# Seven-product form for the output projection and for the whole second MLP product, adding DMAs for low parts, and operand tiles moved by 32 bytes, in a gated two-branch trunk

## The chip, the cores and the metric

The kernel runs on one core of a Trainium2 chip. The metric is the device time of one execution in microseconds (us). Three runs of the kernel before took 847.4, 850.44 and 851.98 us; their median is 850.44 us.

## The reference

One layer over 512 tokens of 1024 channels, all in float32, with a final norm behind it:

```python
h = rmsnorm(x, norm_mix[l])
proj = h @ w_in[l]
zu, zv, zq, zf, zi, zo, g_a, g_b = jnp.split(proj, split_points, axis=-1)
y_a = gmlp_branch(zu, zv, ...) @ w_up_a[l]
y_b = hgrn2_branch(zq, zf, zi, zo, ...) @ w_up_b[l]
mix = jax.nn.sigmoid(g_a) * y_a + jax.nn.sigmoid(g_b) * y_b
x = x + mix @ w_out[l]
h = rmsnorm(x, norm_ffn[l])
x = x + jnp.square(jax.nn.relu(h @ w_ff1[l])) @ w_ff2[l]
...
return rmsnorm(x, final_norm)
```

`w_out` is 1024x1024 and `w_ff2` is 4096x1024. These two products, and the norm between the projection and the MLP, are what the change touches.

## The kernel before

**Precision.** Each float32 operand is split into a high part H and a low part L, both in the type float32r. `split` (L87 to L90) writes H by a copy on ScalarE (ACT, L89) and L = source - H by a subtraction on VectorE (DVE, L90). `mm3` (L106 to L115) then does three matmuls for each pair of blocks: H by H (L113), L by H and H by L (L114, L115), summed in PSUM. `operand` splits a weight tile of 128x1024 into the tiles WH and WL, two rings of NOPER = 5 buffers each; `wload` also loads the tile, in the order of a list (`_plan`), through a ring of four tiles named raw.

**Seven products.** Where a product is cut into 2x2 blocks it can be done in seven block products with sums of blocks before and after, in place of eight. `seven` (L117 to L157) does this for the branch gates and for most of the first MLP product; the loop at L721 to L791 does it for chunks 1 to 3 of the second one. A chunk is eight blocks of 128 hidden channels, and its 168 matmuls of 128x512 are seven products of 24. Its inner function `product` (L748) splits an activation quarter into aH and aL, splits two weight tiles and calls `mm3`. Two of the weight sums, w1 and w3, come from DRAM ready: a DMA from SyncE's queue (SP) writes one quarter and a second DMA, issued by GpSimd (POOL), adds another one:

```python
nc.sync.dma_start(t, rows(*parts[0], k))
if len(parts) > 1:
    nc.gpsimd.dma_start(t, rows(*parts[1], k), accum_op=ALU.add)
```

**Plain products.** The output projection (L612 to L623) and chunk 0 of the second MLP product (L670 to L682) are plain: 192 matmuls of 128x512 each. In the projection the operands mixH and mixL were split tile by tile inside the `upb` loop (L585 to L592); each of the eight results is added to x2 by one DVE addition (L619), squared for the norm on ACT, and in the second half `norm_to_T` (L222 to L235) normalises a token tile, transposes it on TensorE (PE) and splits it into h2H and h2L.

**After the projection** the first MLP product does its first four blocks plainly (L635 to L644), in two halves of 256 tokens, and 14 pairs by `seven`. Then follow chunk 0, chunks 1 to 3 and the final norm.

**Order.** Each engine runs its own instructions in one fixed order, which the framework's list scheduler derives at build time (L876) from the program and the pools. A tile's address comes from the order in which pools hand out tiles.

Of the kernel before, what the change touches and what calls it, by code (L numbers as in the profile page):

```python
# [29 lines left out]
NSLOW = 8  # L30
# [15 lines left out]
def _plan():  # L46
# [15 lines left out]
    for hf in range(2):  # L62
        names += [("out", hf, k) for k in range(4)]
    names += [("ff1", f) for f in range(NF)]
    names += [("ff2", f) for f in range(NSLOW)]
    for c in range(NSLOW // 8, NF // 8):
        names += [("ff2q", c, j, l, k) for j, l in QUARTERS for k in range(2)]
# [4 lines left out]
def trunk_kernel(ctx: ExitStack, tc: tile.TileContext, A: dict, out: bass.AP):  # L72
# [7 lines left out]


# [10 lines left out]
    def operand(src):  # L92
        n = src.shape[-1]
        H = wp.tile([P, 1024], F32R, tag="WH", bufs=NOPER, name="WH")
        L = wp.tile([P, 1024], F32R, tag="WL", bufs=NOPER, name="WL")
        split(src, H[:, :n], L[:, :n])
        return H, L

    def wload(*name):
        return operand(wraw(*name))  # L100
# [81 lines left out]


# [64 lines left out]
    yaL = pya.tile([P, NG, S], F32R, name="yaL")  # L248

# [314 lines left out]
    pt = left2.enter_context(tc.tile_pool(name="pt", bufs=1, side="left", reuse_waits="tile"))  # L564
    ps_g = left2.enter_context(tc.tile_pool(name="ps_g", bufs=1, space=bass.MemoryType.PSUM))
# [17 lines left out]
    mixH = pmix.tile([P, KD, S], F32R, name="mixH")  # L583
    mixL = pmix.tile([P, KD, S], F32R, name="mixL")
    for d in range(KD):  # L585
# [5 lines left out]
        nc.vector.tensor_tensor(sb, part[0][:, d, :], sb, ALU.add)  # L591
        split(sb, mixH[:, d, :], mixL[:, d, :])  # L592
# [9 lines left out]
    pr3 = left2.enter_context(tc.tile_pool(name="pr3", bufs=1, side="left", reuse_waits="tile"))  # L602
    h2H = pr3.tile([P, KD, S], F32R, name="h2H")
# [8 lines left out]
    for hf in range(2):  # L612
        W = [wload("out", hf, k) for k in range(4)]
        cs = slice(hf * 512, (hf + 1) * 512)
        for t in range(NT):
            acc = ps.tile([P, S], F32, tag="acc", bufs=2, name="acc")
            tt = slice(t * P, (t + 1) * P)
            mm3(acc, [((mixH[:, k, tt], mixL[:, k, tt]), blk(W[k // 2], k % 2, 512)) for k in range(KD)])
            nc.vector.tensor_tensor(x2[:, t, cs], x2[:, t, cs], acc, ALU.add)  # L619
            junk = pn.tile([P, S], F32, tag="junk", bufs=1, name="junk")  # L620
            mean_square(junk, x2[:, t, cs], ssq2[:, t, hf:hf + 1])
            if hf == 1:
                norm_to_T(pn, x2[:, t, :], t, ssq2[:, t, :], [gbc2[:, :S], gbc2[:, S:]], h2H, h2L)  # L623
# [3 lines left out]
    pn_stack.close()  # L627
# [34 lines left out]
    eight = [b for pool, tag in ((ps, "hm"), (ps, "acc"), (ps2, "y5"), (ps2, "y3")) for b in banks(pool, tag)]  # L662
    aT, W2 = {}, {}

    def ff2(f, t, hf):
        tt = slice(t * P, (t + 1) * P)
        mm3(eight[2 * t + hf], [((aT[f][0][:, tt], aT[f][1][:, tt]), blk(W2[f], hf, 512))],
            (f == 0, f == NSLOW - 1))

    for f in range(NSLOW):  # L670
        aT[f] = operand(act[f])
        W2[f] = wload("ff2", f)
        if f < NSLOW - 2:
# [14 lines left out]
    ms = po2.tile([P, NT, 2], F32, name="ms")  # L690

    def add_to(l, m, src):

        for i in range(2):
            c = x2[:, 2 * l + i, m * S:(m + 1) * S]
            nc.vector.tensor_tensor(c, c, src[i], ALU.subtract if m else ALU.add)
# [24 lines left out]
    for c in range(NSLOW // 8, NF // 8):  # L721
        one, end = c == NSLOW // 8, c == NF // 8 - 1
        def rows(j, l, k):
            return A["w"][index[("ff2q", c, j, l, k)]]

        def fresh(pool, tag, bufs, *parts):

            ts = [pool.tile([P, 1024], F32, tag=tag, bufs=bufs, name=tag) for k in range(2)]
            for k, t in enumerate(ts):
                nc.sync.dma_start(t, rows(*parts[0], k))  # L730
                if len(parts) > 1:
                    nc.gpsimd.dma_start(t, rows(*parts[1], k), accum_op=ALU.add)
            return ts

        b11 = fresh(wp, "raw", 4, (0, 0))
        w1 = fresh(wp, "raw", 4, (0, 1), (0, 0))
        b22 = fresh(po2, "rawx", 6, (1, 1))
        w4 = fresh(po2, "rawx", 6, (1, 0))  # L740
        w3 = fresh(po2, "rawx", 6, (1, 1), (0, 1))
        a = {(i, j): acts[c][:, 4 * j:4 * j + 4, 256 * i:256 * i + 256] for i in range(2) for j in range(2)}

        def add(x, y):
            for k in range(2):
# [134 lines left out]
```

## Time and profile before

| | |
|---|---|
| median of three runs | 850.44 us |
| the profiled execution | 850.19 us |
| its span, first to last instruction | 848.4 us |
| granted TensorE clock, mean | 0.995 of full speed |
| PE busy | 831.3 us |
| DVE busy | 637.3 us |
| ACT busy | 401.4 us |
| POOL busy | 47.6 us |
| bytes moved by DMA | 92.68 MB |

The page of the profile is one execution. Busy time is summed for each engine; the records of matmuls overlap, because they are pipelined, so how fast PE works is read from the distance between the starts of two matmuls and not from the length of one. Times in the trace count from the first instruction. The stages in it: `upb` ends at 463.0, the projection ends at 509.5, the plain part of the first MLP product at about 534, `seven` at about 676, chunk 0 at about 721, chunks 1 to 3 at about 840.

### The profile page before, as it was taken

Reading aid. Unit: us, or ns where it says so; the run is one execution under the profiler, and the core shown is the slowest. Engines: PE = TensorE matmul, PEld = TensorE weight load, DVE = VectorE, ACT = ScalarE, POOL = GpSimd, SP = SyncE. Lnnn points to the kernel's source line nnn. Section 1 sums busy time; section 2 is a strip of 40 time slices with the busy share of each in tenths; the row PEclk is TensorE's granted clock in tenths of the full one; section 3 lists DMA queues with packets and bytes.
Section 4 is the critical chain, followed back from the end, with each engine's and each line's share of the span. In section 5 each row is a group of like instructions: output and inputs, shape, how many; then the busy total and the mean of one; then the engine's idle time right before and its main releaser. Section 6 shows DMA issues by size and latency. Waiting matters only on the chain.

```text
span 848.4 us, 13369 instructions
## 1 busy us (share of the span) xinstructions
PE 831.3 (98%) x5282; PEld 748.2 (88%) x5282; DVE 637.3 (75%) x1092; ACT 401.4 (47%) x644; POOL 47.6 (6%) x79
## 2 busy tenths in 40 slices
PE   8999999999999999999999999899999999999996
PEld 6989898989889997999988889899999988777884
DVE  6563888979799587788565349877777574899996
ACT  6433434333342335556533333777766642545464
POOL 2000000000001000000000012000000000010103
PEclk9999999999999999999999999999999999999998
DMA  9233212121221122133423412222322285194812
GB/s 330 88 121 110 100 51 75 51 75 51 75 75 50 51 76 75 54 121 106 147 100 122 162 62 100 70 105 101 120 105 101 100 290 182 28 280 101 233 27 99
DMA packets 26912, 92.68 MB, mean 109 GB/s; under 512 B 3361, under 2 KB 3873, under 8 KB 26850
## 3 DMA queue, kind: packets, MB, share of 16 engines
q1 hardware_dynamic: 24546, 84.49, 28.1%
q0 software_dynamic: 1728, 6.29, 4.0%
q10 hardware_dynamic: 576, 1.05, 0.3%
q8 instruction: 41, 0.67, 0.3%
q14 instruction: 21, 0.17, 0.1%
HBM read 89.72 MB, written 2.10 MB: 108 GB/s over the span
## 4 chain that ended last, share of the span: by engine, by line
PE 88%; DMA 4%; DVE 3%; issue 2%; ACT 2%; POOL 0%; SPq 0%; POOLq 0%; ACTq 0%; DVEq 0%
PE acc L114 14%; PE acc L113 14%; PE acc L115 14%; PE prodx L115 5%; PE prodx L113 5%; PE prodx L114 5%; DMA raw<-in_w_dram 4%; PE prodzy L115 4%; PE prodzy L114 4%; PE prodzy L113 4%; PE sp L437 4%; PE hm L115 2%; PE hm L114 2%; PE hm L113 2%; PE y L113 2%
## 5 line engine op out<-in xcount | busy, mean ns | idle before, releaser
L90 DVE TENSOR_TENSOR WL<-raw,WH 128x1024 fp32r<-128x1024 f32 (+1 forms) x134 | 152.0, 1137 | 102.5 <-ACT WH L89 102.0
L89 ACT ACTIVATE WH<-raw 128x1024 fp32r<-128x1024 f32 (+1 forms) x134 | 132.4, 989 | 184.7 <-PE acc L114 68.4
L113 PE MATMUL acc<-WH,hTH 128*128 128x256 f32 x320 | 91.7, 287 | 0.5 <-ACT hTH L89 0.5
L115 PE MATMUL acc<-WH,hTL 128*128 128x256 f32 x320 | 91.6, 286 | 0.0
L114 PE MATMUL acc<-WL,hTH 128*128 128x256 f32 x320 | 90.6, 283 | 0.0
L115 PE MATMUL acc<-hTH,WL 128*128 128x512 f32 x160 | 64.3, 402 | 0.0
L114 PE MATMUL acc<-hTL,WH 128*128 128x512 f32 x160 | 64.1, 401 | 0.0
L113 PE MATMUL acc<-hTH,WH 128*128 128x512 f32 x160 | 64.1, 400 | 0.0
L90 DVE TENSOR_TENSOR WL<-s,WH 128x1024 fp32r<-128x1024 f32 x44 | 53.8, 1222 | 10.5 <-ACT WH L89 9.6
L113 PEld LDWEIGHTS acc<-WH,hTH 128*128 128x128 f32 x320 | 60.4, 189 | 0.7 <-ACT hTH L89 0.7
L115 PEld LDWEIGHTS acc<-WH,hTL 128*128 128x128 f32 x320 | 60.4, 189 | 0.1
L114 PEld LDWEIGHTS acc<-WL,hTH 128*128 128x128 f32 x320 | 60.3, 189 | 0.0
L89 ACT ACTIVATE WH<-s 128x1024 fp32r<-128x1024 f32 x44 | 46.7, 1061 | 14.1 <-PE prodx L114 8.7
L446 DVE COPY_PREDICATED scores<-mask,sp 128x192 f32<-128x192 int32 (+2 forms) x144 | 43.9, 358 | 6.8 <-PE sp L437 6.4
L114 PE MATMUL hm<-WL,aH 128*128 128x512 f32 x96 | 38.1, 397 | 0.0
L115 PE MATMUL hm<-WH,aL 128*128 128x512 f32 x96 | 38.0, 396 | 0.0
L113 PE MATMUL hm<-WH,aH 128*128 128x512 f32 x96 | 37.9, 396 | 0.0
L437 PE MATMUL sp<-QX,K 128*128 128x192 f32 x192 | 35.9, 326 | 0.0
L115 PEld LDWEIGHTS acc<-hTH,WL 128*128 128x128 f32 x160 | 30.1, 188 | 6.4
L114 PEld LDWEIGHTS acc<-hTL,WH 128*128 128x128 f32 x160 | 30.1, 188 | 6.4
L113 PEld LDWEIGHTS acc<-hTH,WH 128*128 128x128 f32 x160 | 30.1, 188 | 6.2
L89 ACT ACTIVATE WH<-rawx 128x1024 fp32r<-128x1024 f32 x24 | 25.1, 1052 | 19.3 <-issue 10.7
(298 smaller groups left out, 2417.1 us busy)
## 6 DMA issues: line engine op xcount, KB each, us to landing
raw<-in_w_dram SPq DMA_DIRECT2D x128, 512.0 KB, 3.5
rawx<-in_w_dram SPq DMA_DIRECT2D x18, 512.0 KB, 8.5
rawx<-in_w_dram POOLq DMA_DIRECT2D x6, 512.0 KB, 6.4
raw<-in_w_dram POOLq DMA_DIRECT2D x6, 512.0 KB, 9.0
x_t<-in_x_dram SPq DMA_DIRECT2D x4, 512.0 KB, 6.1
x<-in_x_dram SPq DMA_DIRECT2D x4, 512.0 KB, 5.7
out_dram<-x ACTq DMA_DIRECT2D x4, 256.0 KB, 2.8
out_dram<-x SPq DMA_DIRECT2D x4, 256.0 KB, 2.4
```

The costliest lines, as they stand in the source:

```text
L89: nc.scalar.activation(H, src, AF.Copy)
L90: nc.vector.tensor_tensor(L, src, H.bitcast(F32), ALU.subtract)
L113: nc.tensor.matmul(acc, ah, bh, start=first and i == 0, stop=False, **kw)
L114: nc.tensor.matmul(acc, ah, bl, start=False, stop=False, **kw)
L115: nc.tensor.matmul(acc, al, bh, start=False, stop=last and i == n - 1, **kw)
L437: nc.tensor.matmul(sp[:, j * 192:(j + 1) * 192].rearrange("p (g c) -> p g c", g=g), K[:, t * P:(t + 1) * P], QX[:, t * g:(t + 1) * g, 1:7, ...
L446: nc.vector.copy_predicated(scv[:, :, i0:i0 + n, :], mv[:, :, x0:x0 + n, :], spv[:, :, x0:x0 + n, :])
```

## The change

- The projection is done in seven products over quarters of one float32 tile `mix` (so no mixH and mixL). The order is p1, p2, p5, p6, p3, p7, p4. The norm of token tile 0 stands ahead of p4, that of tile 1 between p4's two halves, and those of tiles 2 and 3 inside the first half of the plain part of the first MLP product.
- All four chunks of the second MLP product are done in seven products, by the same class `Eighth`. Chunk 0 does p2 behind p1, the others behind p6; the last two are p3 and p4.
- `operand_of` makes the low part of a weight quarter that is no sum in another way: ACT writes H and then -H, and a DMA issued by POOL adds the quarter from DRAM onto -H. It is used for b11, w4 and b22 in the projection, b22 in chunk 0, b11 and b22 in chunks 1 to 3. Each is two tiles, so there are 20 such DMAs; with two tiles each of w1 and w3 in five places there are 20 of the old kind, 40 in all (12 before).
- `shift` takes 32 bytes in four pools, so that ya, the gates' operands, mix's aH and aL, h2 and what lies behind them start 32 bytes further on.

```order
L112 DMA WL_7445<-in_w_dram 128x1024
L112 DMA WL_7450<-in_w_dram 128x1024
L215 DMA w3_7536<-in_w_dram 128x1024
L215 DMA w3_7537<-in_w_dram 128x1024
L112 DMA WL_7547<-in_w_dram 128x1024
L215 DMA w1_7522<-in_w_dram 128x1024
L112 DMA WL_7552<-in_w_dram 128x1024
L215 DMA w1_7523<-in_w_dram 128x1024
```IFF

**How the order moves: DVE at the start of the projection.** Before, from the end of the last `upb` block (acc is its result in PSUM, part the branch sums, WL the low part of a weight tile):

```order
L590 TENSOR_TENSOR part1_3276<-acc_4760,part1_3276 128x512
L591 TENSOR_TENSOR part1_3276<-part0_3275,part1_3276 128x512
L90 TENSOR_TENSOR WL_4952<-raw72_4949,WH_4951 128x1024
L90 TENSOR_TENSOR mixL_4508<-part1_3276,mixH_4507 128x512
L619 TENSOR_TENSOR x2_4794<-x2_4794,acc_4837 128x512
L619 TENSOR_TENSOR x2_4794<-x2_4794,acc_4865 128x512
```

Now, from the same place (X0, X1 are results of p1; E, aL belong to the activations; w1, w4, b22 are weight quarters):

```order
L690 TENSOR_TENSOR part1_3277<-acc_4747,part1_3277 128x512
L691 TENSOR_TENSOR mix_4509<-part0_3276,part1_3277 128x512
L92 TENSOR_TENSOR WL_4918<-w1_4782,WH_4917 128x1024
L260 TENSOR_TENSOR E_4911<-mix_4509 128x1024
L92 TENSOR_TENSOR aL_4867<-mix_4509,aH_4866 128x1024
L231 TENSOR_TENSOR w1_4782<-w1_4782,b22_4788 128x1024
L262 TENSOR_TENSOR mix_4509<-mix_4509 128x4x256
L718 TENSOR_TENSOR x2_4803<-x2_4803,X0_4823 128x512
L92 TENSOR_TENSOR WL_4922<-w1_4783,WH_4921 128x1024
L718 TENSOR_TENSOR x2_4803<-x2_4803,X1_4824 128x512
L231 TENSOR_TENSOR w4_4778<-w4_4778,w1_4782 128x1024
L92 TENSOR_TENSOR aL_4914<-E_4911,aH_4913 128x1024
```

Where DVE had one weight tile to split and then waited for results, it now has 58 instructions from the first of these rows to the last h2L of token tile 1: 27 of 128x1024 elements, 18 of 128x512 that bring a result in, three other sums of 128x512 (for the first MLP product), six halves of normalised tiles and four splits into h2L.

**DVE at the start of the second MLP product.** Before (aT's low parts are WL<-act; one weight tile and one activation tile for 24 matmuls):

```order
L90 TENSOR_TENSOR WL_7277<-act0_5183,WH_7276 128x512
L765 TENSOR_TENSOR act2_5185<-act2_5185 128x4x256
L90 TENSOR_TENSOR aL_7573<-act1_5184,aH_7572 128x1024
L90 TENSOR_TENSOR WL_7283<-raw111_7280,WH_7282 128x1024
L90 TENSOR_TENSOR WL_7311<-act0_5183,WH_7310 128x512
L90 TENSOR_TENSOR WL_7317<-raw112_7314,WH_7316 128x1024
L90 TENSOR_TENSOR WL_7345<-act0_5183,WH_7344 128x512
```

Now:

```order
L92 TENSOR_TENSOR WL_7290<-w4_7227,WH_7289 128x1024
L718 TENSOR_TENSOR x2_4803<-x2_4803,hm0_7214 128x512
L260 TENSOR_TENSOR E_7321<-act0_5179 128x1024
L92 TENSOR_TENSOR WL_7294<-w4_7228,WH_7293 128x1024
L262 TENSOR_TENSOR act0_5179<-act0_5179 128x4x256
L92 TENSOR_TENSOR aL_7286<-act0_5179,aH_7285 128x1024
L263 SCALAR_TENSOR_TENSOR act0_5179<-E_7321,act0_5179 128x4x256
L92 TENSOR_TENSOR aL_7324<-E_7321,aH_7323 128x1024
L718 TENSOR_TENSOR x2_4803<-x2_4803,hm1_7215 128x512
L274 SCALAR_TENSOR_TENSOR act0_5179<-act0_5179 128x4x256
```

The first row behind the last result of the first MLP product (act3) is the first one shown. Twelve instructions of 128x1024 and two of 128x512 now stand ahead of the low part of w1 (WL_7328), which p5's second matmul of its first group reads; before, two instructions stood ahead of each 24 matmuls.

**POOL's queue at the border from chunk 0 to chunk 1.** Before, the adding DMAs at the border from chunk 2 to chunk 3 and ahead of it (two each for w1 and w3):

```order
L732 DMA raw_7765<-in_w_dram 128x1024
L732 DMA raw_7766<-in_w_dram 128x1024
L732 DMA rawx_7779<-in_w_dram 128x1024
L732 DMA rawx_7780<-in_w_dram 128x1024
L732 DMA raw_8058<-in_w_dram 128x1024
L732 DMA raw_8059<-in_w_dram 128x1024
L732 DMA rawx_8072<-in_w_dram 128x1024
L732 DMA rawx_8073<-in_w_dram 128x1024
```

Now, at the border from chunk 0 to chunk 1 (WL_7445 and WL_7450 are low parts for p3 of chunk 0, WL_7547 and WL_7552 those for p1 of chunk 1):

```order
L112 DMA WL_7445<-in_w_dram 128x1024
L112 DMA WL_7450<-in_w_dram 128x1024
L215 DMA w3_7536<-in_w_dram 128x1024
L215 DMA w3_7537<-in_w_dram 128x1024
L112 DMA WL_7547<-in_w_dram 128x1024
L215 DMA w1_7522<-in_w_dram 128x1024
L112 DMA WL_7552<-in_w_dram 128x1024
L215 DMA w1_7523<-in_w_dram 128x1024
```

Eight adding DMAs stand behind each other, and the two that p1 of chunk 1 waits for are the fifth and the seventh.

## Rows read from the trace of the kernel before

**Rows 1.** The page: busy time, share of the span and instructions of each engine.
```profile
PE 831.3 (98%) x5282; PEld 748.2 (88%) x5282; DVE 637.3 (75%) x1092; ACT 401.4 (47%) x644; POOL 47.6 (6%) x79
```

**Rows 2.** The page: the chain that ended last, share of the span by engine.
```profile
PE 88%; DMA 4%; DVE 3%; issue 2%; ACT 2%; POOL 0%; SPq 0%; POOLq 0%; ACTq 0%; DVEq 0%
```

**Rows 3.** Windows: from:to us; their length, busy us (instructions); granted clock, DMA share, GB/s.
```profile
463.00:509.50 46.50, 46.50 (x209) 37.72 (x208) 20.36 (x26) 16.07 (x27) 4.59 (x10) 1.00 0.32 114
...
520.00:545.00 25.00, 22.66 (x188) 22.25 (x188) 22.21 (x24) 15.63 (x23) 0.00 (x0) 1.00 0.18 63
545.00:676.00 131.00, 131.00 (x1104) 131.00 (x1103) 97.70 (x128) 89.75 (x144) 0.00 (x0) 1.00 0.30 103
676.00:721.00 45.00, 45.00 (x206) 37.51 (x206) 27.43 (x30) 17.85 (x23) 3.72 (x4) 1.00 0.71 229
721.00:770.00 49.00, 47.98 (x203) 37.62 (x203) 44.99 (x45) 23.91 (x24) 3.49 (x4) 1.00 0.59 160
770.00:815.00 45.00, 45.00 (x194) 36.23 (x194) 42.14 (x44) 26.95 (x27) 3.50 (x4) 1.00 0.52 141
```

**Rows 4.** Timeline, PE, `upb` loop, then chunk 2: start us, length us, instruction.
```profile
437.83 0.39 PE L113 MATMUL acc<-ybH,WH 128*128 128x512 f32 x1
...
445.99 0.39 PE L113 MATMUL acc<-ybH,WH 128*128 128x512 f32 x1
...
795.74 0.40 PE L113 MATMUL hm<-WH,aH 128*128 128x512 f32 x1
...
801.10 0.40 PE L115 MATMUL hm<-WH,aL 128*128 128x512 f32 x1
```

**Rows 5.** Timeline, PE, inside `seven` of the first MLP product.
```profile
560.46 0.28 PE L113 MATMUL prodx<-t2H,WH 128*128 128x256 f32 x1
...
561.75 0.28 PE L115 MATMUL prodx<-t2H,WL 128*128 128x256 f32 x1
...
562.95 0.28 PE L113 MATMUL prodzy<-h2H,WH 128*128 128x256 f32 x1
...
564.63 0.28 PE L115 MATMUL prodzy<-h2H,WL 128*128 128x256 f32 x1
```

**Rows 6.** Timeline, PE: first matmul of the projection and first after it.
```profile
463.00 0.39 PE L113 MATMUL acc<-WH,mixH 128*128 128x512 f32 x1
...
509.51 0.40 PE L113 MATMUL acc<-h2H,WH 128*128 128x256 f32 x2
510.17 0.66 PE L232 MATMUL pt<-ident,xn 128*128 128x128 f32 x4 [0.26 <-DVE h2L L90]
```

**Rows 7.** Timeline, DVE: end of `upb`, `norm_to_T`, chunk 1.
```profile
463.20 0.69 DVE L590 TENSOR_TENSOR part<-acc,part 128x512 f32<-128x512 f32 x1 [2.29 <-PE acc L115]
...
499.38 1.42 DVE L228 SCALAR_TENSOR_TENSOR xn<-x,rr_n,g_ffn 128x512 f32<-128x512 f32 x2 [1.90 <-POOL rr_n L209]
500.71 1.28 DVE L90 TENSOR_TENSOR h2L<-pt,h2H 128x512 fp32r<-128x512 f32 x2
...
728.40 0.68 DVE L696 TENSOR_TENSOR x<-x,hm 128x512 f32<-128x512 f32 x1
729.00 2.35 DVE L746 TENSOR_TENSOR raw<-raw,rawx 128x1024 f32<-128x1024 f32 x2
731.27 0.68 DVE L696 TENSOR_TENSOR x<-x,hm 128x512 f32<-128x512 f32 x1
```

**Rows 8.** The page: DMA queues (packets, MB, share of 16 engines).
```profile
q1 hardware_dynamic: 24546, 84.49, 28.1%
q0 software_dynamic: 1728, 6.29, 4.0%
```

**Rows 9.** The page: DMA issues (count, KB each, median us from issue to landing).
```profile
rawx<-in_w_dram SPq DMA_DIRECT2D x18, 512.0 KB, 8.5
rawx<-in_w_dram POOLq DMA_DIRECT2D x6, 512.0 KB, 6.4
raw<-in_w_dram POOLq DMA_DIRECT2D x6, 512.0 KB, 9.0
```

More of the change, by code (lines that the diff above doesn't have):

```diff
@@ L79, in trunk_kernel, with shift @@
     ps = ctx.enter_context(tc.tile_pool(name="ps", bufs=1, space=bass.MemoryType.PSUM))
+    def shift(pool):
+        pool.tile([P, 8], F32, name="shift")
     def wraw(*name):
@@ L90, in split, with operand, operand_of @@
         nc.vector.tensor_tensor(L, src, H.bitcast(F32), ALU.subtract)
-    def operand(src):
-        n = src.shape[-1]
+    def operand(src, quarter=False):
+        n = 1024 if quarter else src.shape[-1]
         H = wp.tile([P, 1024], F32R, tag="WH", bufs=NOPER, name="WH")
         L = wp.tile([P, 1024], F32R, tag="WL", bufs=NOPER, name="WL")
-        split(src, H[:, :n], L[:, :n])
+        if quarter:
+            split(src, *(p.rearrange("p (k t) -> p k t", k=4) for p in (H, L)))
+        else:
+            split(src, H[:, :n], L[:, :n])
+        return H, L
+    def operand_of(src, *dram):
+        H = wp.tile([P, 1024], F32R, tag="WH", bufs=NOPER, name="WH")
+        L = wp.tile([P, 1024], F32R, tag="WL", bufs=NOPER, name="WL")
+        nc.scalar.activation(H, src, AF.Copy)
+        nc.scalar.activation(L, H.bitcast(F32), AF.Copy, scale=-1.0)
+        for d in dram:
+            nc.gpsimd.dma_start(L, d, accum_op=ALU.add)
         return H, L
@@ L689, in trunk_kernel @@
     X, Z, Y5, Y3 = banks(ps, "hm"), banks(ps, "acc"), banks(ps2, "y5"), banks(ps2, "y3")
[L690 to L696, printed above, removed]
+    ms = po2.tile([P, NT, 4], F32, name="ms")
     def squares(l, m):
@@ L719, in finish @@
             nc.scalar.dma_start(out[t * P:(t + 1) * P, m * S:(m + 1) * S], early)
[L721 to L741, printed above, removed]
-        a = {(i, j): acts[c][:, 4 * j:4 * j + 4, 256 * i:256 * i + 256] for i in range(2) for j in range(2)}
-        def add(x, y):
-            for k in range(2):
-                nc.vector.tensor_tensor(x[k], x[k], y[k], ALU.add)
-        def product(acc, src, w, first, last):
-            H = po2.tile([P, 4, 256], F32R, tag="aH", bufs=3, name="aH")
-            L = po2.tile([P, 4, 256], F32R, tag="aL", bufs=3, name="aL")
-            split(src, H, L)
-            W = [operand(w[k]) for k in range(2)]
-            for i in range(2):
-                mm3(acc[i], [((H[:, k, i * P:(i + 1) * P], L[:, k, i * P:(i + 1) * P]),
-                              blk(W[k // 2], k % 2, 512)) for k in range(4)], (first, last))
-        product(X, a[0, 0], b11, True, False)
+    for c in range(NF // 8):
+        one, end = c == 0, c == NF // 8 - 1
+        a = {(i, j): acts[c][:, 4 * j:4 * j + 4, 256 * i:256 * i + 256] for i in range(2) for j in range(2)}
+        e = Eighth(a, "w_ff2", c, po2, ("b11", "w4" if one else "w1"),
+                   adding=("b22",) if one else ("b11", "b22"))
+        e.p1(X, one)
         add_to(0, 0, X)
-        e = po2.tile([P, 4, 256], F32, tag="E", bufs=1, name="E")
-        nc.vector.tensor_tensor(e, a[1, 1], a[1, 0], ALU.subtract)
-        product(Y5, e, w1, one, end)
+        if one:
+            e.p2(Z, True, False)
+        e.p5(Y5, one, end)
         if end:
@@ L764, in trunk_kernel @@
             add_to(1, 1, Y5)
-        nc.vector.tensor_tensor(a[1, 0], a[0, 0], a[1, 0], ALU.subtract)
-        nc.vector.scalar_tensor_tensor(a[0, 0], e, -1.0, a[0, 0], ALU.mult, ALU.subtract)
-        add(w1, b22)
-        product(X, a[0, 0], w1, False, False)
+        e.p6(X)
         add_to(0, 1, X)
-        product(Z, a[0, 1], w4, one, end)
+        if not one:
+            e.p2(Z, False, end)
         if end:
@@ L774, in trunk_kernel @@
             scaled(0, 0)
-        add(w4, w1)
-        product(X, a[1, 0], w3, False, False)
+        e.p7(X)
         add_to(1, 1, X)
@@ L780, in trunk_kernel @@
             scaled(1, 1)
-        nc.vector.scalar_tensor_tensor(a[0, 1], a[0, 1], -1.0, a[0, 0], ALU.mult, ALU.subtract)
-        product(Y3, a[0, 1], b22, one, end)
+        e.p3(Y3, one, end)
         if end:
```

162 lines of the change are left out of this document (114 added, 48 removed).

## Prediction

> **What bounds the kernel now.** I read the busy shares first: PE is busy 831.3 us and DVE 637.3 us [rows 1]. The chain of waits that ended last says the same, 88% of it is PE [rows 2]. So the time is PE's matmuls, and a change pays if it takes matmuls away or makes them start closer together, as long as the others keep up. That is a matter of each stage, so I read the windows next [rows 3]: in the projection DVE works 20.4 of 46.5 us, in chunk 0 of the second MLP product 27.4 of 45 us, but in chunks 1 to 3, which have the seven-product form already, 45.0 of 49 and 42.1 of 45 us. There DVE is almost as full as PE. The change puts that form into the two stages where DVE was half idle. The last thing I read is the distance between starts of matmuls, since their records overlap [rows 4, 5].
>
> An execution's time is its span and 1.8 us around it (850.19 against 848.4). The sum is made against 850.2 us, which is 0.2 us under the median. A measurement of this kernel can tell about 0.5%, here 4.25 us, from no change.
>
> **What is taken from PE.** In the `upb` loop and in chunk 0 matmuls of 128x512 follow each other by (445.99 - 437.83) / 36 = 0.2267 us; where the activation operand is aH or aL, by (801.10 - 795.74) / 23 = 0.2330 us [rows 4]. In `seven` the step is (561.75 - 560.46) / 11 = 0.1173 us with t2 and (564.63 - 562.95) / 14 = 0.1200 us with h2 [rows 5]. Shape, type and clock are the same, so what differs is where the operands lie: the slow pairs are those of 128x512 whose two addresses differ modulo 64 bytes, and those of 128x256 whose addresses agree. By the tile addresses of the changed kernel nearly all its matmuls of 128x512 behind the gates agree and all of 128x256 differ. So:
> - chunk 0 goes from 192 to 168 matmuls: 24 x 0.2267 = 5.4 us less;
> - chunks 1 to 3: 504 x 0.0063 = 3.2 us less; the 96 matmuls on ya: 0.6 us less;
> - 1152 matmuls of the first MLP product lose 0.0027 us each by these rows, 3.1 us; their starts are rounded to 0.01 us, which leaves 1.8 to 4.4 us. I take 2.5 us, on the low side, because the gain is the difference of two rounded numbers.
>
> A rule speaks against the three shift terms. The Trainium skill ("TensorE: Matmul & The Clock Gate", "Step-by-step: what each phase is for") says that the streaming operand and the weight load have read ports of their own, so that loading weights takes nothing from a running matmul; by it addresses would not matter, the terms would be zero, and the sum 6.3 us higher. The rows disagree, with 0.2267 against 0.2330 us for the same work, and I follow them.
>
> **The projection.** PE's own work falls from 192 matmuls to 168 x 0.2267 = 38.1 us, and 16 transposes add some 1.7 us: 39.8 us from the end of `upb` to the first plain group of the next stage. It was 509.51 - 463.00 = 46.5 us [rows 6]. But DVE can't do its part in 39.8 us. It begins 0.2 us after the last `upb` result (463.20, rows 7 show the step of each kind) and has 58 instructions in a row before the h2L that the second matmul of the next stage reads: 27 of 128x1024 at (731.27 - 729.00) / 2 = 1.135, 21 of 128x512 at 0.60, six halves xn at 0.71, four h2L at 0.64 [rows 7]. That is 30.6 + 12.6 + 4.3 + 2.6 = 50.1 us without any wait. With 1 us for waits inside (a row of xn waited 1.9 us for its factor, [rows 7]; here other work stands between) the stage takes 0.2 + 50.1 + 1.0 = 51.3 us: 4.8 us **more** than before, though PE has 6.7 us less to do. PE gets there about 11.5 us late, in steps; bounds are 10 (no wait inside) and 13. The low parts of p1, p2 and p3 come by DMA and not through DVE; without that it would be six times 1.135 us worse. p1's and p2's are asked for while `upb` runs; p3's have the lateness of DVE as cover. I cost them at nothing (if they came late: up to 9.0 us, [rows 9]).
>
> **The first MLP product.** Between 520 and 545 us PE was idle 25 - 22.66 = 2.3 us [rows 3]. Now norms of tiles 2 and 3 stand between plain groups, and DVE has little else there; I take this wait as gone (2.3 us less; bounds 0 and 2.3).
>
> **Chunk 0.** DVE comes to it right after the last result of `seven`. The first result of p1 is there 12 matmuls later, at 2.7 us plus 0.3. From then on it has two instructions at 0.60 and 12 at 1.135 before the low part of w1: it is ready at 3.0 + 1.2 + 13.6 = 17.8 us. PE reaches the matmul that reads it after p1's 24 matmuls, 12 of `seven` between p1's halves, p2's 24 and two of p5: 12 x 0.12 + 50 x 0.2267 = 12.7 us. So PE waits 5.1 us there. That DVE is well ahead until then (97.7 of 131 us in `seven`, [rows 3]) doesn't help, since its second row waits for p1's first result. Bounds 3, if some of the twelve are done while it waits, and 7, if w1's loads and adds come late.
>
> **The border to chunk 1.** An adding DMA costs more than a plain one: 12 of them took 4.0% of 848.4 us, or 2.8 us of all sixteen engines each, while 0.524 MB of the plain queue took 28.1% x 848.4 x 0.524 / 84.49 = 1.5 us [rows 8]. From issue to landing it takes 6.4 to 9.0 us [rows 9]. The low part of chunk 1's first b11 tile can be started when the fifth tile ahead of it in the ring is free, at p7's end; PE needs it 47 matmuls = 10.7 us later, and it stands behind two adds for w3. One copy (1 us), 6.4 to 9.0 us, and up to 2 x 2.8 us behind the two: 7.4 to 15.6 us. So the wait is 0 to 5 us; the second tile is alike, with one add ahead. I take 3 us, as the two adds ahead of it wait for plain loads that start late. For the later borders I take 1 us together (0 to 4): the order is the same but the adds are asked for earlier. They replace 49 - 48.0 = 1.0 us that PE waited in chunk 1 [rows 3].
>
> **Work at no cost.** The 20 copies of -H are 20 us on ACT, which works 24 to 27 of 45 to 49 us in these chunks [rows 3]. DMA is busier: a chunk has ten plain loads and eight adds, 10 x 1.5 + 8 x 2.8 = 37.4 us by the means of [rows 8], against 38.1 us for its 168 matmuls; With four adds the same sum is 26.2 us, where the windows show 0.52 x 45 = 23.4 to 0.59 x 49 = 28.9 us; scaled by these the new chunk has 33 to 41 us. That is nearly full. It is the ground of the slow rival.
>
> **The sum.** 850.2 - 5.4 - 3.2 - 0.6 - 2.5 + 4.8 - 2.3 + 5.1 + 3 + 1 - 1.0 = 849.1 us. PE's work falls by some 18 us, and waits for DVE and DMA take nearly all of it back. I forecast **849 us**, no change that can be told.
>
> **The rivals.**
> - *Faster: the MLP keeps up.* Only the projection is late; chunk 0 and the borders are not, because a late PE gives DVE and the adds time that my walk counts twice (each wait moves all that follows). 849.1 - 5.1 - 3 - 1 = 840 us. For it: POOL and ACT are idle most of the time. Against it: DVE's order at chunk 0 has no slack. Chance 0.24.
> - *Faster: DVE keeps up in the projection too*, if its instructions overlap more than 1.135 us apart. 840 - 11.5 = 828.5 us. Against it: that step is the same wherever two stand back to back. Chance 0.12.
> - *Slower: the adds saturate.* One queue takes eight adds per chunk; when they follow each other by more than 38.1 / 8 = 4.8 us, each of chunks 1 to 3 ends with the queue and not with PE. At 5.5 us, between 2.8 and the 6.4 us of a landing, a chunk takes 44 us, 5.9 us more: 849.1 + 3 x 5.9 - 4 = 863 us. For it: the work per chunk above. Against it: before, four adds per chunk left PE only 1 us of waits. Chance 0.18.
> - *The shift does nothing*, because the step follows the tile and not its address: the change then doesn't do what it says, and 849.1 + 6.3 = 855 us. Against it: every tile of either kind fits the rule of addresses. Chance 0.08. It is what the Trainium skill's rule above would give.
>
> **How the numbers follow.** My forecast has 0.38, and it lies wholly within 0.5% (846.2 to 854.7). Faster has 0.24 + 0.12 = 0.36; slower 0.18 + 0.08 = 0.26. The range takes in 840 and 855 with the bounds of the border terms, and leaves out half of the second and half of the third rival: 835 to 860 us.
>
> **What would show it.** If I am right, the profile after has 0.227 us between matmuls of 128x512 in the projection and in all chunks; DVE nearly full from 463 to 514 us and PE idle some 11 us there, waiting for aL, WL and h2L by DVE; about 5 us of PE idle early in chunk 0; and a few us at the next border on a DMA into WL. I am wrong if PE is idle less than 6 us in the projection, if the waits on WL by DMA pass 8 us in all, or if matmuls still stand 0.233 us apart.

## The result and the profile after

The changed kernel takes 874.21 us (median of four runs, 873.68 to 877.58), where the kernel before took 849.02 us in runs beside it. The ratio is 1.03, with a 95% interval of 1.0268 to 1.0332: **slower by 3%**, outside the range of the forecast. The profiled execution has a span of 872.2 us, against 848.4 before, and a mean granted clock of 0.982.

From the page of the kernel after: busy time by engine, the two main DMA queues, the chain that ended last, and the issues of adding DMAs (count, KB each, median us from issue to landing).

```profile
PE 829.2 (95%) x5234; PEld 741.4 (85%) x5234; DVE 658.2 (75%) x1106; ACT 437.1 (50%) x674; POOL 76.4 (9%) x107
...
q1 hardware_dynamic: 25122, 86.59, 27.8%
q0 software_dynamic: 5760, 20.97, 12.6%
...
PE 79%; DMA 10%; DVE 5%; issue 3%; ACT 2%; POOL 1%; SPq 0%; POOLq 0%; DVEq 0%; ACTq 0%
...
w<-in_w_dram POOLq DMA_DIRECT2D x20, 512.0 KB, 11.4
WL<-in_w_dram POOLq DMA_DIRECT2D x20, 512.0 KB, 9.1
```

PE is busy 2 us less than before [rows 1], not 18: busy time also counts matmuls that run at a lower clock, and the shorter step that was forecast for the second MLP product did not come (see the section on the prediction). The chain that ended last is 79% PE now, and 10% DMA where it was 4% [rows 2]. The adding queue q0 moves 20.97 MB in place of 6.29 and takes 12.6% of the engines' time [rows 8]; one add now lands after 9.1 and 11.4 us where it was 6.4 and 9.0 us [rows 9].

Where the time came from is read by stage, between the same matmuls in both traces (in us; the forecast's terms put to the stage that they were meant for):

| stage | before | after | forecast | measured |
|---|---|---|---|---|
| start to the first matmul of the projection | 463.0 | 459.1 | -0.6 | -3.9 |
| from there to the first matmul on h2L | 47.6 | 54.5 | +4.8 | +6.9 |
| first MLP product, to its last matmul | 168.8 | 167.8 | -4.8 | -1.0 |
| second MLP product, to its last matmul | 160.9 | 182.5 | -0.5 | +21.6 |
| final norm and output | 8.1 | 8.3 | 0 | +0.2 |

Windows of the kernel after (the columns are those of [rows 3]), in the projection, in `seven`, and from chunk 0 to the border of chunks 1 and 2:

```profile
480.00:500.00 20.00, 17.19 (x64) 13.15 (x63) 15.23 (x19) 11.06 (x16) 6.85 (x8) 0.83 0.45 108
500.00:520.00 20.00, 14.11 (x74) 12.42 (x73) 18.93 (x26) 8.06 (x16) 5.80 (x7) 0.83 0.37 129
545.00:676.00 131.00, 131.00 (x1125) 131.00 (x1124) 100.10 (x130) 92.77 (x148) 0.00 (x0) 1.00 0.30 105
...
690.00:720.00 30.00, 23.29 (x92) 17.85 (x91) 26.25 (x25) 17.96 (x18) 6.00 (x7) 0.94 0.86 219
720.00:740.00 20.00, 16.19 (x56) 12.53 (x56) 8.30 (x8) 5.29 (x5) 2.59 (x3) 0.83 1.06 254
740.00:770.00 30.00, 27.70 (x118) 21.61 (x117) 25.67 (x26) 20.47 (x21) 2.59 (x3) 1.00 0.51 139
770.00:790.00 20.00, 18.36 (x77) 13.92 (x76) 13.32 (x14) 7.98 (x9) 4.43 (x5) 1.00 1.05 266
```

In `seven` nothing waits, as before. In the projection PE is busy 14 to 17 of 20 us at a granted clock of 0.83, in chunk 0 (690 to 720) 23 of 30 us at 0.94, and behind it (720 to 740) 16 of 20 us at 0.83. At the borders (720 to 740 and 770 to 790) the DMA engines' share is 1.06 and 1.05: they are full there. The long windows of [rows 3] show no more than 0.59 for the seven-product chunks before, but over 20 us the kernel before came near to full as well, ahead of its chunk 2, and PE lost only 0.4 us there:

```profile
745.00:765.00 20.00, 19.64 (x85) 15.50 (x84) 19.43 (x20) 10.08 (x11) 3.32 (x4) 1.00 0.92 274
```

Waits of PE in the kernel after (what PE waited for, us in all, times, longest), the five longest of the program's second half:

```profile
PE y L130 <- DMA WL<-in_w_dram: 7.8, 4, 2.7
PE y L129 <- ACT WH L91: 5.2, 2, 4.3
PE acc L130 <- DVE h2L L92: 4.2, 1, 4.2
PE hm L130 <- DMA WL<-in_w_dram: 4.2, 2, 3.8
PE Y L130 <- DMA WL<-in_w_dram: 2.8, 1, 2.8
```

Three of the five are adding DMAs into WL: 14.8 us. The first and the last of these three are p3's, the product that reads the quarter b22: one wait in each of the four chunks (7.8 us) and one in the projection (2.8 us). The other is mostly p1's, at the border to chunk 1 (3.8 us). The second entry, on ACT, is mostly w1 of chunk 0 (4.3 us), which ACT could not copy before its own adding DMA had landed. Only the third is DVE, as forecast, in the projection.

**The projection.** PE's timeline of the kernel after: the first matmul of the projection, the stall in p3 (Y is its result), and the two first matmuls of the next stage:

```profile
459.09 0.39 PE L129 MATMUL X<-WH,aH 128*128 128x512 f32 x1
...
482.63 0.39 PE L129 MATMUL Y<-WH,aH 128*128 128x512 f32 x1
485.82 0.79 PE L130 MATMUL Y<-WL,aH 128*128 128x512 f32 x1 [2.81 <-DMA WL<-in_w_dram]
486.41 0.63 PE L131 MATMUL Y<-WH,aL 128*128 128x512 f32 x1
486.84 0.63 PE L129 MATMUL Y<-WH,aH 128*128 128x512 f32 x1
...
508.85 0.50 PE L129 MATMUL acc<-h2H,WH 128*128 128x256 f32 x2 [0.95 <-ACT h2H L91]
513.59 0.58 PE L130 MATMUL acc<-h2L,WH 128*128 128x256 f32 x1 [4.24 <-DVE h2L L92]
```

The stage ends with DVE, as forecast, at 513.59 - 459.09 = 54.5 us instead of 51.3. The low part of p3 came 2.8 us late by DMA. Its add was issued late, at 480.28, and landed 5.5 us later. Behind that stall the matmuls follow each other by 0.427 us instead of 0.227 us for 13 steps. That is 512 columns at 1.2 GHz, the lower of the two levels; the granted clock is 0.50 from 485.0 to 491.8. DVE, which had no time to lose, stands still behind it:

```profile
488.17 1.23 DVE L92 TENSOR_TENSOR WL<-w,WH 128x1024 fp32r<-128x1024 f32 x1
494.00 1.23 DVE L92 TENSOR_TENSOR WL<-w,WH 128x1024 fp32r<-128x1024 f32 x1 [4.60 <-ACT WH L91]
...
512.85 1.28 DVE L92 TENSOR_TENSOR h2L<-pt,h2H 128x512 fp32r<-128x512 f32 x2
```

Its gap of 4.60 us at 494.00 (ACT had to wait for PE's slow matmuls to free a weight buffer) is the difference to the forecast and a bit more. The stall of 4.24 us ahead of h2L costs the next stage too: the granted clock is 0.50 again from 512.3 to 519.1, the matmuls of 128x256 follow each other by 0.213 us instead of 0.117 us, and that takes about 2 us. That is most of why the first MLP product gained 1.0 us and not the 4.8 us of the forecast; its waits fell by 1.6 us where 2.3 were forecast, and three more matmuls of chunk 0 stand ahead of its end.

**Chunk 0 and the border.** DVE's timeline of the kernel after, at the low part of chunk 0's w1:

```profile
693.70 1.22 DVE L262 TENSOR_TENSOR act<-act 128x1024 f32<-128x1024 f32 x1
695.85 1.23 DVE L92 TENSOR_TENSOR WL<-w,WH 128x1024 fp32r<-128x1024 f32 x1 [0.92 <-ACT WH L91]
```

PE stood from 691.4 to 697.1, but for two matmuls. The wait that ended last is that for w1's adding DMA, but DVE, which had worked without a gap since 681.7, was ready for w1 only 0.92 us earlier. With w1 there in time its low part would have come at 696.15, and PE would still have stood some 4.2 us. So the 5.1 us that the forecast put down to DVE's order are nearly right, and the add came on top with 0.9 us. POOL's timeline at the border to chunk 1, and PE's at the first of its low parts:

```profile
710.00 0.86 POOL L112 DMA_DIRECT2D WL<-in_w_dram  x1 [15.09 <-ACT WL L110]
711.89 0.86 POOL L112 DMA_DIRECT2D WL<-in_w_dram  x1 [1.04 <-ACT WL L110]
714.56 0.85 POOL L215 DMA_DIRECT2D w<-in_w_dram  x1 [1.81 <-DMA w<-in_w_dram]
716.60 0.86 POOL L215 DMA_DIRECT2D w<-in_w_dram  x1 [1.18 <-DVE WL L92]
718.69 0.86 POOL L112 DMA_DIRECT2D WL<-in_w_dram  x1 [1.23 <-ACT WL L110]
```

```profile
733.99 0.68 PE L130 MATMUL hm<-WL,aH 128*128 128x512 f32 x1 [3.81 <-DMA WL<-in_w_dram]
734.47 0.63 PE L131 MATMUL hm<-WH,aL 128*128 128x512 f32 x1
734.89 0.63 PE L129 MATMUL hm<-WH,aH 128*128 128x512 f32 x1
```

The add for chunk 1's first low part is issued at 718.69 and PE gets it at 733.99, 15.3 us later; then matmuls step by 0.427 us again. The chain of waits (start, length, what) has it as one piece:

```profile
718.69 15.26 DMA WL<-in_w_dram
```

It is the fifth add in 9 us, and SP had issued nine of the ten plain loads for the next chunk between 701.8 and 717.3. The eight adds of this border land in their order, at 718.99, 722.53, 726.30, 730.19, 733.95, 736.47, 738.92 and 741.40: 3.5 to 3.9 us apart at first, while plain loads land too (up to 730.4), and 2.5 us apart at the end. The fifth stood behind three that were still under way.

p3's two adds are the first two of such a group of eight in each chunk. From issue to landing in chunks 0, 1 and 3:

```profile
DMA to landing us min/median/max: 9.0/9.8/10.6
DMA to landing us min/median/max: 10.2/11.1/12.0
DMA to landing us min/median/max: 5.5/5.5/5.6
```

In chunk 3, behind which no other chunk is loaded, they take 5.5 us, and beside the next chunk's plain loads about twice that. This compares stretches of one trace; no run moved the plain loads themselves.

In all, steps at the low level cost PE about 2.5 us more than the usual step in the projection, 2 us in the first MLP product and 5.5 us in the second. In the second MLP product PE waits 19.4 us, where 9.1 us (5.1 + 3 + 1) were forecast.

### The profile page after: what moved, and what is told of

It reads as the page before. It is cut to its first block, busy times and chain, and to the rows that moved or that the text cites. A ratio compares the mean times of both kernels' runs of the same rounds, so it can differ in the third digit from the quotient of the medians.

```text
span 872.2 us, 13422 instructions
## 1 busy us (share of the span) xinstructions
PE 829.2 (95%) x5234; PEld 741.4 (85%) x5234; DVE 658.2 (75%) x1106; ACT 437.1 (50%) x674; POOL 76.4 (9%) x107
## 3 DMA queue, kind: packets, MB, share of 16 engines
q0 software_dynamic: 5760, 20.97, 12.6%
q10 hardware_dynamic: 576, 1.05, 0.3%
## 4 chain that ended last, share of the span: by engine, by line
PE 79%; DMA 10%; DVE 5%; issue 3%; ACT 2%; POOL 1%; SPq 0%; POOLq 0%; DVEq 0%; ACTq 0%
PE acc L129 12%; PE acc L130 12%; PE acc L131 12%; DMA WL<-in_w_dram 5%; PE prodx L131 5%; PE prodx L129 5%; PE prodx L130 5%; DMA w<-in_w_dram 4%; PE sp L536 4%; PE prodzy L130 4%; PE prodzy L131 3%; PE prodzy L129 3%; PE hm L130 2%; DVE WL L92 2%; PE hm L129 2%
## 5 line engine op out<-in xcount | busy, mean ns | idle before, releaser
L92 DVE TENSOR_TENSOR WL<-raw,WH 128x1024 fp32r<-128x1024 f32 x100 | 110.8, 1108 | 74.4 <-ACT WH L91 73.9
L91 ACT ACTIVATE WH<-raw 128x1024 fp32r<-128x1024 f32 x100 | 96.5, 966 | 124.2 <-PE acc L130 50.4
L91 ACT ACTIVATE WH<-w 128x1024 fp32r<-128x1024 f32 x48 | 49.3, 1052 | 58.3 <-DMA w<-in_w_dram 19.7
L92 DVE TENSOR_TENSOR WL<-w,WH 128x1024 fp32r<-128x1024 f32 x48 | 58.0, 1223 | 17.7 <-ACT WH L91 17.7
L130 PE MATMUL hm<-WL,aH 128*128 128x512 f32 x120 | 48.7, 406 | 4.2 <-DMA WL<-in_w_dram 4.2
L215 POOL DMA_DIRECT2D w<-in_w_dram x20 | 18.8, 974 | 339.4 <-DVE aL L92 172.8
L131 PE MATMUL hm<-WH,aL 128*128 128x512 f32 x120 | 48.1, 401 | 0.0
L129 PE MATMUL hm<-WH,aH 128*128 128x512 f32 x120 | 47.3, 403 | 0.0
L718 DVE TENSOR_TENSOR x<-x,hm 128x512 f32<-128x512 f32 x32 | 21.9, 686 | 23.6 <-PE hm L131 23.5
## 6 DMA issues: line engine op xcount, KB each, us to landing
w<-in_w_dram POOLq DMA_DIRECT2D x20, 512.0 KB, 11.4
```

Source lines behind the costliest of these rows:

```text
L91: nc.scalar.activation(H, src, AF.Copy)
L92: nc.vector.tensor_tensor(L, src, H.bitcast(F32), ALU.subtract)
L129: nc.tensor.matmul(acc, ah, bh, start=first and i == 0, stop=False, **kw)
L130: nc.tensor.matmul(acc, ah, bl, start=False, stop=False, **kw)
L131: nc.tensor.matmul(acc, al, bh, start=False, stop=last and i == n - 1, **kw)
L215: nc.gpsimd.dma_start(t, A["w"][index[(kind, c, *parts[1], k)]], accum_op=ALU.add)
```

## Experiments

All ratios are to the kernel before in runs beside them. Where a diff changes `adding`, the low parts are made by DVE's subtraction.

### The moves alone, and the change without them

e1 is the kernel before with the moves alone: a small tile behind `yaL`, at the start of `pt` and `pr3` and behind `mixL`, and a wider `ms`.

```diff
     yaL = pya.tile([P, NG, S], F32R, name="yaL")
+    pya.tile([P, 8], F32, name="shift")
...
-    ms = po2.tile([P, NT, 2], F32, name="ms")
+    ms = po2.tile([P, NT, 4], F32, name="ms")
```

e2 is the changed kernel without the small tiles.

```diff
     def shift(pool):
-        pool.tile([P, 8], F32, name="shift")
+        return
```

> The kernel before with the 32-byte moves alone (ya, the gates' operands, mix, h2 and the first MLP product's operands, and aH, aL of chunks 1 to 3); every engine's order is that of before. If the distance between matmuls follows the two operand addresses: 192 + 504 + 96 matmuls of 128x512 at 0.0063 us less each, 5.0 us, and 1152 of 128x256 at up to 0.0027 us, up to 3.1 us; so 841 to 844 us, faster by 0.6 to 1.0%. If the step belongs to the tiles and not to their addresses: 849 us, no change.

Measured: 843.39 us, ratio 0.994 (0.9923 to 0.9957), as expected if addresses count. The moves are worth 5.6 us of 849 by themselves.

> The changed kernel without the moves in ya, the gates' operands, mix's aH and aL, and h2; every engine's order is that of the changed kernel. If addresses count, 96 matmuls on ya (0.6 us) and 1152 of 128x256 (up to 3.1 us) grow; the 168 of the projection (1.1 us) grow under DVE's work there and cost nothing: 875 to 879 us. If they don't count: 874 us.

Measured: 878.83 us, 4.6 us above the changed kernel (ratio 1.0354, 1.0334 to 1.0374, against 1.0268 to 1.0332). So addresses count, with the order of every engine unchanged. But the size was right for a partly wrong reason: in chunks 1 to 3 of e1 the step had not changed. PE's timeline of e1 in chunk 2, 20 steps apart:

```profile
781.30 0.39 PE L113 MATMUL hm<-WH,aH 128*128 128x512 f32 x1
...
785.97 0.39 PE L115 MATMUL hm<-WH,aL 128*128 128x512 f32 x1
```

That is 4.67 / 20 = 0.2335 us, as before the move [rows 4], though both addresses now agree modulo 64. They were 0 (aH) and 192 (WH) modulo 256. In the changed kernel aH is at 0 as well, and the 648 matmuls on it in the second MLP product step by 0.233 us, those of chunk 0 too. The last two runs below follow this up.

### Adding DMAs for low parts

e3 is the changed kernel with both of these edits, e4 with the second alone.

```diff
-    proj = Eighth(quarters, "w_out", 0, pmix, ("b11", "w4"), 2, ("b11", "w4", "b22"))
+    proj = Eighth(quarters, "w_out", 0, pmix, ("b11", "w4"), 2, ())
...
-                   adding=("b22",) if one else ("b11", "b22"))
+                   adding=())
```

> The changed kernel with every low part made by DVE's subtraction, none by an adding DMA (20 adds in place of 40). Theory A, the queue of adding DMAs is what costs: the waits of PE on a DMA into WL, 14.8 us in the trace of the changed kernel, and most of the steps at the slower clock behind them go; DVE gets 20 x 1.135 us more, of which the projection's six lie on its path (6.8 us), so 855 to 866 us. Theory B, the seven-product form itself leaves DVE too much in chunk 0 and the projection, and the adds only fill its shadow: DVE's added work makes it worse, 876 to 890 us.

> The changed kernel with the low parts of the second MLP product alone made by DVE; the projection keeps its six adds. Theory A: the waits on WL by DMA in chunks 0 to 3 (12.0 us with their slow clock some 20 us) go and DVE has 37.8 us for 38.1 us of PE in chunks 1 to 3, which costs 0 to 8 us: 852 to 862 us, some 4 us under the kernel without any such add. Theory B: 872 to 884 us.

Measured: 862.36 us (ratio 1.0157, 1.0137 to 1.0177) and 861.68 us (1.0155, 1.0136 to 1.0174). Taking the 14 adds for low parts out of the second MLP product gives 12.5 us back; the theory that the low adds are late (A in the texts on record) holds there. The six in the projection are worth no more than 0.7 us, the difference of the two kernels, though DVE has 6.8 us less to do with them; one reason is the late add with the slow steps behind it, and how much else there is was not followed up. What is left is plain in the second kernel: all waits of PE in its second MLP product above 1.3 us are one entry (columns as above), both times for a w1:

```profile
PE y L129 <- ACT WH L91: 9.8, 2, 5.5
```

The chain of waits (start, length, what) at the second of them, at the start of chunk 1's p5:

```profile
719.56 10.62 DMA w<-in_w_dram
...
730.28 1.06 ACT WH L91
```

The adding DMA for w1 landed 10.6 us after its issue, though it had no add for a low part beside it.

### Chunk 0 in the order of the others

```diff
-        e = Eighth(a, "w_ff2", c, po2, ("b11", "w4" if one else "w1"),
+        e = Eighth(a, "w_ff2", c, po2, ("b11", "w1"),
...
-        if one:
-            e.p2(Z, True, False)
...
-        if not one:
-            e.p2(Z, False, end)
+        e.p2(Z, one, end)
```

`near` names the two quarters that sit in the ring of the first MLP product's weights and can be loaded while that product still runs. The run e5 has this edit on top of e4's, e8 has it alone.

> The kernel without low adds in the MLP, and chunk 0 of the second product done in the order of the other chunks, with w1 and not w4 in the ring of the first product's weights; no low adds in the projection either. Theory C, w1's place costs: in chunk 0 w1 can be loaded only when the first product's operands are gone, and w4, which p4 uses last, holds the two tiles that chunk 1's w1 needs. The two waits of PE on ACT for w1 with the slow clock behind them (6.6 and 8.3 us in the trace without low adds in the MLP) go: 861.7 - 14.9 = 847, and 2 us more for the projection's lows by DVE: 847 to 852 us. Rival, DVE is the limit in chunk 0 whatever w1 does (the forecast's 5.1 us, then 37.8 us of work for 38.1): 855 to 862 us.

> The changed kernel with chunk 0 in the order of the others and w1 in the weights' ring, all other adds kept. If the adds for low parts are late by themselves (theory A): the waits on WL in chunks 0 to 3 stay, some 12 us and 4 us of slow clock, and only w1's 6.8 us go: 864 to 869 us. If they were late because w1 held them up in the one queue: 847 to 856 us.

The text on record is wrong in one thing: e5 kept the projection's six low adds, like e4, so its number is to be held against 861.7 - 14.9 = 847 without the 2 us. Measured: 853.69 us (1.0055, 1.0036 to 1.0074) and 869.96 us (1.0255, 1.023 to 1.0281). The edit was worth 8.0 us of the 14.9: both waits went, but a new one of 5.1 us came at the border from the first to the second MLP product (next run). It moves w1 and puts p2 back behind p6 at once, which changes DVE's order too, so the 8.0 us can't be put down to w1's place alone. With the low adds kept, the same edit gives only 4.2 us, and the two kernels differ by 16.3 us in nothing but how those 14 low parts are made. Each of the adds brings a copy of -H on ACT with it and spares DVE a subtraction; in the second MLP product of e8 PE waits 9.8 us for adds into WL, and in that of e5 it has no such wait; both have the wait at the border, 4.6 us in e8 and 5.1 us in e5. So the adds are late by themselves, not because w1 held them up.

### The projection alone, and the second MLP product alone

e6 is e5 with the plain projection of the kernel before (its operands moved by 32 bytes). e7 has the seven-product projection, but chunk 0 plain.

> The same second MLP product as in the kernel before this one, but with the plain projection of the kernel before (operands moved by 32 bytes). If theory C holds, its head is that of the kernel with the moves alone, and the second product takes 672 x 0.2267 = 152.3 us and 0 to 4 us of waits in place of 159.5 us there: 843.4 - 3 to 843.4 - 7, so 836 to 841 us, faster than both kernels. Rival, chunk 0 in seven products costs as much as it saves (DVE): 843 to 850 us.

> Seven products for the projection (no low adds), plain chunk 0, chunks 1 to 3 as before, all moved by 32 bytes. If DVE's 50 us in a row set the projection's end, it costs what the traces show: 53.6 to 56.1 us from the end of upb to the second matmul of the next stage, against 46.8 with the moves alone, less 1.3 us in the stage behind: 849 to 852 us. If the loss in the projection were only the late adds and the clock behind them, none of which is here for p3: 840 to 844 us.

Here too the text is wrong about e7: it kept the projection's six low adds. Measured: 848.34 us (0.9996, 0.9985 to 1.0007), the rival's case, and 850.86 us (1.0026, 1.001 to 1.0041). Against the moves alone, 843.39 us, the seven-product chunk 0 costs 4.9 us in this form and the seven-product projection 7.5 us. ACT's timeline of e6 at the border shows why the first is no gain:

```profile
677.79 1.06 ACT L92 ACTIVATE WH<-w 128x1024 fp32r<-128x1024 f32 x1 [6.17 <-DMA w<-in_w_dram]
678.75 0.36 ACT L174 ACTIVATE act<-prodx 128x256 f32<-128x256 f32 x1
```

ACT's second copy of w1 waits 6.17 us for its adding DMA, and the last result of the first MLP product (L174), which frees a PSUM bank for PE, stands behind it in ACT's order.

> Plain projection, moved operands, seven products for all of the second MLP product without low adds; in chunk 0 w1 sits in the first product's weight ring (so it is loaded and added early), p2 comes second as in the changed kernel, w4 is the first tile of the new pool and the final norm's gain is loaded in chunk 1. In the trace of the kernel with w1 early and p5 second, ACT stood 6.2 us at the border waiting for w1's second adding DMA, with the last result of the first product behind it in its order, and PE lost 5.5 us and 1.6 us of slow clock. In this order ACT takes those results first. Theory C (w1's place and the wait on its add are what chunk 0 costs, DVE's order costs little): 848.3 - 7 + 0 to 2 = 841 to 843 us, as fast as or faster than the moves alone. Rival, the forecast's own walk (DVE gives w1's low part 5 us late in this order, however early w1 lands): 845 to 849 us.

e9 is e6 with p2 back ahead of p5 in chunk 0, and w1 still among the quarters loaded early:

```diff
+        if one:
+            e.p2(Z, True, False)
         e.p5(Y5, one, end)
...
-        e.p2(Z, one, end)
+        if not one:
+            e.p2(Z, False, end)
```

In e9 w4 is also the first tile of its pool, and the final norm's gain is loaded in chunk 1. Measured: 847.87 us (0.9986, 0.9975 to 0.9996), by its number the rival's case. The 6 us on ACT are gone, but ACT waits for w4, and DVE's row for w1 stands behind:

```profile
679.49 1.06 ACT L92 ACTIVATE WH<-w 128x1024 fp32r<-128x1024 f32 x1 [1.54 <-DMA w<-in_w_dram]
```

w4's tile is in a pool that opens when the first product's operands are gone; its load was issued at 670.5 and ACT could start at 679.5. DVE would have held PE up without that too: it works without a gap from 674.7, and the low part of w4's first tile, which p2 needs, comes out of that row at 682.4, where PE was done with p1 at 678.0. No run shows chunk 0 with DVE's order alone.

Chunk 0 in seven products saves 24 matmuls, 5.4 us. 144 of its 168 matmuls step by 0.233 us and not by 0.227 us, which takes back 1.0 us, and PE waits 6.8 us in the second MLP product of e6 and 5.5 us in that of e9, most of it at the entrance, with 1.6 us of slow steps behind it in either. That is more than was saved.

> Seven products in the projection alone as in the run so named, but the four DVE sums of weight quarters (w1 with b22, w4 with w1) are left out, so the projection's result is not the reference's. If DVE's instructions in a row set the end of the projection, the second matmul of the next stage comes 4 x 1.135 = 4.5 us earlier, 3 to 4.5 us of which reach the end: 846 to 848 us, against 850.9 with the sums. If the late low part of p3 by its adding DMA and the slow clock behind it set it: 850 to 851 us, no change.

```diff
         def add(self, x, y):
-            for k in range(2):
+            for k in range(0 if self.kind == "w_out" else 2):
```

Measured: 845.62 us (0.996, 0.9945 to 0.9974), 5.2 us less than with the sums. PE's timeline, first matmul of the projection and first on h2L, with the sums (e7) and without (e10):

```profile
461.29 0.39 PE L130 MATMUL X<-WH,aH 128*128 128x512 f32 x1
...
515.89 0.58 PE L131 MATMUL acc<-h2L,WH 128*128 128x256 f32 x1 [4.29 <-DVE h2L L93]
```

```profile
461.40 0.39 PE L130 MATMUL X<-WH,aH 128*128 128x512 f32 x1
...
510.63 0.58 PE L131 MATMUL acc<-h2L,WH 128*128 128x256 f32 x1 [4.28 <-DVE h2L L93]
```

The stage takes 54.6 and 49.2 us, 5.4 us less for 4.5 us of DVE's work; the other 0.9 us are gaps in DVE's row, 4.7 us with the sums and 3.8 us without. So the end of the projection is set by DVE's row, its work and the gap that the late add of p3 leaves in it. The sums are left out of the result, and p3's adds are issued earlier with them gone, so the gap and the work were not told apart by separate runs.

### Which addresses

> The moves alone, with aH and aL of chunks 1 to 3 moved 64 bytes further, so that their address is 64 modulo 256 where that of WH is 192 modulo 256; order unchanged. With the 32-byte move they were at 0 modulo 128, WH at 64, and the step stayed at 0.2333 us though both agree modulo 64. If the fast step needs addresses that agree modulo 128: 0.227 us a matmul there, 504 x 0.0063 = 3.2 us less than the moves alone, 840 us. If it needs them to agree modulo 256, or depends on something else: 843 to 844 us.

> The same with aH and aL at 192 modulo 256, as WH. If addresses must agree modulo 128 or modulo 256: 840 us. If the step doesn't follow addresses but the tiles or the DVE and ACT traffic of those chunks: 843 to 844 us.

e11 and e12 are e1 with `ms` wider still: 8 in place of 4 in e11, as here, and 16 in e12.

```diff
-    ms = po2.tile([P, NT, 4], F32, name="ms")
+    ms = po2.tile([P, NT, 8], F32, name="ms")
```

Measured: 844.46 us (0.9942, 0.992 to 0.9963) and 842.34 us (0.9924, 0.9907 to 0.9942). PE's timeline in chunk 2, 21 steps apart in e11 and 19 in e12:

```profile
781.54 0.40 PE L115 MATMUL hm<-WH,aL 128*128 128x512 f32 x1
...
786.42 0.40 PE L115 MATMUL hm<-WH,aL 128*128 128x512 f32 x1
```

```profile
785.54 0.39 PE L114 MATMUL y<-WL,aH 128*128 128x512 f32 x1
...
789.85 0.39 PE L113 MATMUL hm<-WH,aH 128*128 128x512 f32 x1
```

The first is as expected without the fast step; the second lies between the two cases expected. The steps are 4.88 / 21 = 0.2324 and 4.31 / 19 = 0.2268 us. With aH at 0, 64 and 192 modulo 256 and WH at 192 the step is 0.2335, 0.2324 and 0.2268 us: in these runs the fast step comes with addresses that agree modulo 256, and agreement modulo 64 is not enough. From the last matmul of the first MLP product to the last of the second, the trace of e1 has 159.5 us and that of e12 156.4 us, 3.1 us less, which is the expected size; of the whole time only 1.1 us is seen in the medians, no clear difference. e12 is the fastest kernel here, 0.8% under the kernel before, and it has none of the new seven-product stages.

## Why the prediction was wrong

- **p3's low parts, "I cost them at nothing", and "For the later borders I take 1 us together".** This is the step that failed: the forecast had no wait for the adds that p3 reads. Of the 14.8 us that PE waits for adds into WL, p3 has 10.6 us, 2.8 in the projection and 7.8 in the four chunks. The wait that did get a price of its own, 3 us for chunk 1's first low part, measured 3.8 us. Without the adds for low parts in the second MLP product 12.5 us come back (e4), 16.3 us with chunk 0 reordered (e8 against e5). The forecast priced an add by medians, 6.4 to 9.0 us [rows 9]; beside the plain loads of the next chunk p3's first adds took 9.0 us and more, and the fifth in a row 15.3 us. The medians hid that the same had been seen before: at the border to chunk 2 of the kernel before, one of four such adds took 12.8 us, at a cost to PE of at most 0.4 us. The slow rival had the right place, but its point of decision, adds more than 4.8 us apart over a whole chunk, is not what happened: at the border to chunk 1 they land 2.5 to 3.9 us apart, over a chunk there is time enough (0.51 DMA share from 740 to 770), and the engines are full (1.06 and 1.05) only for the 20 us at a border, when all of the next chunk's loads and adds are asked for at once.
- **"So PE waits 5.1 us there" (chunk 0).** Measured 5.2 us up to p5's low part. DVE's walk holds, with some 4.2 us by itself; the rest is w1, which comes late as well, as the upper bound of the forecast allowed for. What it did not look at is why: in chunk 0 it can be loaded only when the first product's operands are gone, and w4 in its place holds the two tiles that chunk 1's w1 needs, where PE waits a second time in e4. Moving w1 and p2 gave 8.0 us (e5).
- **"The stage takes ... 51.3 us" (projection).** Right in kind and sign, and the walk of DVE's order holds: 54.5 us, with a 4.6 us gap of DVE that comes from the late add; four sums less on DVE give 5.4 us (e10). What was wrong is the zero for p3's low part. PE idle is 9.8 us there, where 11 were forecast.
- **The clock had no term.** Around stalls of 1.9 to 4.8 us the granted clock fell to its lower level six times ahead of the program's last matmul, for some 10 us of extra step time in all (0.83 in three windows, against 1.00 in every window of [rows 3]). A stall was costed at its own length.
- **The shift terms.** Forecast 6.3 us, measured 5.6 us for the moves alone and 4.6 us for leaving them out of the changed kernel; but the rule behind it (modulo 64) was wrong, and the 3.2 us for chunks 1 to 3 did not come until the addresses agreed modulo 256 (e12). The sign of being wrong that the forecast named, matmuls still 0.233 us apart, is there in all four chunks of the changed kernel. The gates gained what those chunks didn't: that stage is 130.4 us with the moves and 133.0 without. By the rule of the Trainium skill that was weighed here ("TensorE: Matmul & The Clock Gate", "Step-by-step: what each phase is for": separate read ports for the two operands), as the forecast read it, addresses would not matter. Three runs show that they do: the same matmuls in the same order step by 0.2335, 0.2324 or 0.2268 us.
- **The saving of matmuls** was right in their number, but in chunk 0 it is 4.4 us and not 5.4, as their step grew, and none of it reached the end: chunk 0 pays more than that, most of it at its entrance (e6, e9), and the projection's 5.4 us and more go to DVE (e7: 7.5 us above the moves alone).

Put together from the runs: 874.2 us, less 12.5 for the low adds, 8.0 for w1's place and p2's, 5.4 for the projection and 4.9 for chunk 0, is the 843.4 us of the moves alone; each of these terms is the difference of two kernels that stand next to each other in the chain from the changed kernel over e4, e5 and e6 to e1.

## What to carry to other kernels

A product in fewer block products trades matmuls for sums and splits on another engine: before it is made, walk that engine's instructions from the last result it needs to the first matmul that needs it, since its share over a whole stage hides the pile at the stage's entrance. A transfer that replaces an instruction is priced in the stretch where all other transfers of the next stage are asked for, and by the longest landing there, not by a median over the program. And when operands of equal work step at different rates, compare their addresses with a large enough modulus, and try the move by itself.

## What was not expected of the hardware

- The step of a 128x512 matmul depends on the two operands' SBUF addresses modulo 256: in chunks 1 to 3 it is 0.2268 us where they agree (e12), 0.2324 us at 64 against 192 (e11), 0.2335 us at 0 against 192 (e1). That is not all there is to it: in the changed kernel both are at 192 in the end of p3 of the projection (8 steps from 491.95) and in the first half of p1 of chunk 0 (11 steps from 677.35), and the step is 0.231 us there.
- The step of the 128x256 matmuls in `seven` also takes one of two values for a whole stage, 0.1167 or 0.1178 us, between kernels whose order and addresses in that stage are the same: in the first MLP product e1 runs at 0.1178 and e12 at 0.1167, in the gates e3 at 0.1178 and e5 at 0.1167. That is 1% of a stage. What chooses the value was not found.
- An adding DMA of 512 KB took 2.75 us of all sixteen engines (12.6% of 872.2 us for 40 of them; 2.8 us for the 12 before [rows 8]), while its landing time in the changed kernel went from 5.3 to 15.3 us. Adds that stood in a row landed 2.5 us apart, and 3.5 to 3.9 us apart beside plain loads.
